# Hybrid mLSTM/HGRN2 decoder step on one core: Values' pieces placed by ScalarE, sample rows' output turned by VectorE, gates' sums in one product, margins for states, C batch split

## The chip, the cores and the metric

One core of a Trainium2 chip runs the whole layer as one program. The metric is the device time of one execution in microseconds (us). The engines are TensorE (PE; its weight loads are listed apart as PEld), VectorE (DVE), ScalarE (ACT), GpSimd (POOL) and SyncE (SP), whose queue issues nearly all transfers.

## The reference

One decoder layer is computed for 256 prompt tokens and for 8 samples of 8 tokens each, 320 tokens in all, with the same weights. Two mixers read one input projection; everything is in fp32.

```
proj = jnp.einsum('btd,de->bte', x, w_in)
(ml_q, ml_k, ml_v, ml_i, ml_f, ml_o, hg_q, hg_f, hg_i, hg_g, gate_a, gate_b) = jnp.split(proj, offs, axis=-1)
...
ig = (ml_i.astype(f32) + b_ig.astype(f32)).transpose(0, 2, 1)
lf = jax.nn.log_sigmoid(ml_f.astype(f32) + b_fg.astype(f32)).transpose(0, 2, 1)
h, C, n, m = _mlstm(q, k, v, ig, lf, C0, n0, m0)
h = _unheads((h - mu) * lax.rsqrt(var + LN_EPS)) * ml_norm_g
branch_a = h * jax.nn.sigmoid(ml_o)
...
o, S = _hgrn2(hq, jnp.log(f), 1.0 - f, _heads(hg_i, HG_HEADS), S0)
o = _unheads(o * lax.rsqrt(jnp.mean(jnp.square(o), axis=-1, keepdims=True) + LN_EPS)) * hg_norm_g
branch_b = o * jax.nn.silu(hg_g)
ya = jnp.einsum('btv,vd->btd', branch_a, w_branch_a)
yb = jnp.einsum('btv,vd->btd', branch_b, w_branch_b)
merged = jax.nn.sigmoid(gate_a) * ya + jax.nn.sigmoid(gate_b) * yb
x1 = _layernorm(DEEPNORM_ALPHA * x + jnp.einsum('btd,de->bte', merged, w_out), ln1_g, ln1_b)
hid = jnp.square(jax.nn.relu(jnp.einsum('btd,df->btf', x1, w_up)))
y = _layernorm(DEEPNORM_ALPHA * x1 + jnp.einsum('btf,fd->btd', hid, w_down), ln2_g, ln2_b)
```

The mLSTM has 4 heads (key width 256, value width 512), the HGRN2 mixer 8 heads (128 and 256). The final matrix states C and S are outputs as well, for the prompt (from zero) and for each sample (from a given state).

## The kernel before

All values are kept transposed, features on the 128 partitions and the 320 tokens along the row (256 prompt tokens, then 64 sample tokens). The dense projections are 304 tiles of 128 output features. A tile is 48 matmuls that add up in one PSUM bank: 16 slices of the contraction, three matmuls each, because weights and inputs are split into a high and a low part of type fp32r (high times high, high times low, low times high). Weights stream through three raw buffers `wr` of 512 KB, two units to a tile; ScalarE copies a unit to its high part `wh` and VectorE subtracts that to get `wl` (line 501), three prepared buffers in all. In the later stages tile `bb` gives five more pairs. TensorE runs these tiles one after the other (`run_main`).

Everything else is side work, written as generators (`m_...` for the mLSTM, `h_...` for HGRN2, `ev_...` for what is done with a finished tile). A planner (`Sched`) fixes each engine's order ahead of time, while the program is built: it keeps an estimated clock for each engine, and after every three matmuls of a tile it lets each generator put its next instruction into an engine's queue if its inputs should be there by then, up to 900 ns of side work on TensorE at a time. Estimated costs are written at the yields (`act(n)`, `dve(n)`, `pe_f(n)`); an event's `t` is the time at which something is thought to be there. On the chip each engine works its list in that order and waits on semaphores for inputs.

The pieces that the change touches:

- `rows` (line 782) makes the mLSTM's gates. Eight input and forget gates were summed in four partial rows by matmuls; two products with a 4-column selector (`sel`, lines 799 and 800) add these up, input gates in one bank, forget gates in another.
- `turn` (line 1152) turns a head's values (or HGRN2's inputs) from feature rows to token rows. It makes 24 VectorE transposes of 32x32 blocks a call, 16 for the prompt (line 1163) and 8 for the samples (line 1166), each reading 32 partitions and writing 32 others. It is called by `m_V` for 4 heads and by `h_i` for 8.
- `m_sample` and `h_out` end with a head's sample rows. The normalised output (`hb[:, 2, :]`, 128 by 512, or `on[:, 2, :]`, 128 by 256; only 64 of the 128 rows are real, 16 in every 32) is transposed on TensorE, four (line 1219) or two (line 1647) blocks of 128x128, copied from PSUM by ScalarE into token order and sent to a scratch tensor in DRAM (`hL`, `oL`) by one transfer. Prompt rows go another way already: a VectorE transpose in place and four transfers (`place`) that put 32x32 blocks where they belong.
- `ev_o` and `ev_hg` fetch these rows back (`fetch`) and multiply a gate by the norm's weight and by the row, one VectorE instruction each (lines 1704 and 1741).
- `m_states` and `h_load` load the samples' states, 256 and 512 KB a transfer; `m["parts"]` and `m["sat"]` are the times at which TensorE's batch that reads them (`PE_C`, `PE_H`) may be planned.
- `m_C` (line 1116) makes the prompt's final C after the last tile: for each head and half a batch of six matmuls of 512 columns, put into the queue as one piece. The first batch may go before the last norm's sums are done; the others wait for `ln[1]["fin"]`, which `ln_final` posts after its products for the sum and the sum of squares (lines 1842 and 1843). `ln_scale` and `y` then finish the output: 16 subtractions (line 1981) and 16 multiplications (line 1988) on VectorE, a ScalarE pass each, and transfers of `y`. `h_S` makes the final S, whose results are copied by ScalarE and VectorE (line 1616) and sent in four transfers.

Of the kernel before, what the change touches and what calls it, by code (L numbers as in the profile page):

```python
# [8 lines left out]
F32 = mybir.dt.float32  # L9
# [11 lines left out]
TOK = 320  # L21
# [56 lines left out]

C_ID, C_TRI, C_BM, C_SEL, C_SC, C_END = 0, 128, 256, 320, 328, 968


def constants():
# [8 lines left out]
    for r in range(4):  # L91
        c[r::32, C_SEL + r] = 1.0
        c[r + 4::32, C_SEL + 4 + r] = 1.0
    start = np.zeros(TOK, bool)
# [30 lines left out]
PE_OUT = 200.0  # L125
PART = 122.0
PE_LAT = 450.0

# [124 lines left out]
def acq(pool, n=1):  # L253
    return ("acq", pool, n)
# [63 lines left out]
class Program:  # L318
    def __init__(self, tc, nc, d, pools):
# [15 lines left out]
        self.f1 = p.tile([128, 10240], F32, name="f1", tag="f1")  # L335
        self.f2 = p.tile([128, 5232], F32, name="f2")
        self.f3 = p.tile([128, 5120], F32, name="f3", tag="f3")
# [29 lines left out]
    def carve(self):  # L367
# [58 lines left out]
        self.ats = Pool([self.ats0])  # L426
        self.sg = Pool([Part(self.f2, 4912)(320), self.tst2])
        B = Part(self.f2, 4176)
# [7 lines left out]
    def carve_h(self):  # L436
        C = self.Part(self.pool.tile([128, 5120], F32, name="f3h", tag="f3"))
        qz = C(256)
        self.hqz = Pool([qz])
        self.hyk = Pool([C(128)])  # L440
        for x in (qz, self.ats0, self.hkz0.bitcast(F32), *(y[0:64, 2, :] for y in self.it2)):
            self.nc.gpsimd.memset(x, 0.0)
        X, R = self.Part(self.pool.tile([128, 4096], F32R, name="rxb", tag="rx")), self.Part(self.ra)
        self.bah = Slices([(X if j < 12 else R)(TOK) for j in range(KT)])
        self.bal = Slices([R(TOK) for _ in range(KT)])
        now = self.s.t["pe"]
        self.hs.free += [(now, C(2048)), (now, self.hs3)]
        self.sb.free += [(now, C.three(4, 256)) for _ in range(2)]
        self.sg.free += [(now, self.f2[:, 4912:5232]), (now, self.late[0])]
        self.sr.free.append((now, self.late[1]))  # L450
        self.ld = Pool(self.late[2:])
# [330 lines left out]
    def rows(self, b):  # L782
# [10 lines left out]
        emg = row(128)  # L793
        sel = self.cst[:, C_SEL:C_SEL + 8]
# [9 lines left out]
        yield ("dve", dve(T, True), lambda: v.tensor_scalar(fx, p2[0:4, :T], bf, None, ALU.add))  # L804
        yield rel(self.sbank, p1)
        yield rel(self.sbank, p2)
        yield ("act", act(T), lambda: self.A(ax, fx, AF.Abs))
# [308 lines left out]
    def m_C(self, h):  # L1116
# [8 lines left out]
        for c in range(2):  # L1125
            if h or c:
                yield wait(self.ln[1]["fin"])
            b = yield acq(self.mbank)
            yield ("pe", 6 * pe_r(512), lambda: [self.mm(
                b, k.rearrange("p x s k -> p (x s k)")[:, 512 * x + 256 * c + 128 * s:512 * x + 256 * c + 128 * s + 128], w[:, y, s, :], start=n == 0, stop=n == 5)  # L1130
                for n, (s, x, y) in enumerate((s, x, y) for s in range(2) for x, y in ((0, 0), (0, 1), (1, 0)))])
            if c == 1:
# [19 lines left out]
    def turn(self, to, x):  # L1152

        v = self.nc.vector
        n = x.shape[1]
        for a in range(4):
            p = slice(32 * a, 32 * a + 32)
            col = lambda y: y.rearrange("p (c a k) -> p a c k", a=4, k=32)[:, a]
            for b in range(4):
                q = slice(32 * b, 32 * b + 32)  # L1160
                i = x[p, :, 0:NP_].rearrange("p c (i b k) -> p b i c k", b=4, k=32)[:, b]
                o = to[q, 0:2, :].rearrange("p i (c a k) -> p a i c k", a=4, k=32)[:, a]
                yield ("dve", dve_t(64 * n), lambda: v.transpose(o, i))  # L1163
            for b in range(2):
                o, i = col(to[64 + 32 * b:96 + 32 * b, 2, :]), x[p, :, NP_ + 32 * b:NP_ + 32 * b + 32]
                yield ("dve", dve_t(32 * n), lambda: v.transpose(o, i))

# [5 lines left out]
    def m_sample(self, h):  # L1173
# [42 lines left out]
        yield rel(self.sm, dn)  # L1216
        b = yield acq(self.sbank)
        for j in range(4):
            yield ("pe", PE_T, lambda: nc.tensor.transpose(b[:, 128 * j:128 * j + 128], hb[:, 2, 128 * j:128 * j + 128], self.ident))  # L1219
# [9 lines left out]
        yield rel(self.tst, o)  # L1229
        yield wait(m["hb_"])  # L1230
# [17 lines left out]
    def m_states(self, h):  # L1248
# [3 lines left out]
        for n in range(2 * NB):  # L1252
# [3 lines left out]
            m["cbs"].append(cb)  # L1256
            m["parts"][n].t = t
        yield post(m["ld"])
# [222 lines left out]
    def h_i(self, h):  # L1481
# [11 lines left out]
        hi, lo = vst[64:128, 0, :], vst[0:64, 0, :]  # L1493
        yield ("act", act(256), lambda: self.A(hi, it[64:128, 2, :]))
        yield ("dve", dve(256), lambda: v.tensor_tensor(lo, it[64:128, 2, :], hi.bitcast(F32), ALU.subtract))
        yield post(m["I"])
# [8 lines left out]
    def h_load(self, h):  # L1505
# [11 lines left out]
        m["sat"] = Ev()  # L1517
        m["sat"].t = t

# [102 lines left out]
    def h_out(self, h):  # L1622
# [21 lines left out]
        yield rel(self.at, at)  # L1644
        b = yield acq(self.sbank)
        for j in range(2):
            yield ("pe", PE_T, lambda: nc.tensor.transpose(b[:, 128 * j:128 * j + 128], on[:, 2, 128 * j:128 * j + 128], self.ident))  # L1647
        o = yield acq(self.ho)
        for j in range(2):
            yield ("act", act(64, True), lambda: self.A(by_row(o, 64 * j, False), by_row(b, 128 * j, True)))  # L1650
        yield rel(self.sbank, b)
        yield ("sp", 620, lambda: self.dma(
            self.oL[h].rearrange("(j p) t -> p j t", p=128), o[:, 0:128].rearrange("p (j t) -> p j t", t=64)))
        for j in range(2):
            yield post(self.oT_ev[2 * h + j])
        yield wait(self.later())
        yield rel(self.ho, o)
        yield wait(done)
# [34 lines left out]
    def fetched(self, kind, j):  # L1693
        yield wait(self.got[kind, j])
        return self.met[kind, j]

    def ev_o(self, j, c, b):
        v = self.nc.vector
# [4 lines left out]
        x = yield from self.fetched("o", j)  # L1703
        yield ("dve", dve(TOK, ptr=1), lambda: v.scalar_tensor_tensor(g, g, self.vec[:, V_MLG + j:V_MLG + j + 1], x, ALU.mult, ALU.mult))
        yield rel(self.ld, x)
# [26 lines left out]
    def ev_hg(self, j, c, b):  # L1732
# [7 lines left out]
        x = yield from self.fetched("hg", j)  # L1740
        yield ("dve", dve(TOK, ptr=1), lambda: v.scalar_tensor_tensor(g, g, self.vec[:, V_HGG + j:V_HGG + j + 1], x, ALU.mult, ALU.mult))
        yield rel(self.ld, x)
# [354 lines left out]
```

## Time and profile before

| | |
|---|---|
| median of 3 runs | 2295.86 us (2295.74 to 2296.64) |
| the profiled execution | 2296.11 us |
| its span | 2294.3 us |
| TensorE busy, instructions | 2285.9 us, 15592 |
| VectorE busy | 1458.0 us (64%) |
| ScalarE busy | 1036.4 us (45%) |
| transfers | 424.95 MB, mean 185 GB/s |

The span is the time that the profile covers; 1.8 us of the execution lie around it. A matmul of plain fp32 appears as two instructions (two passes), one of fp32r and a TensorE transpose as one. Matmuls overlap: the time that one takes from the stream is read from the distance between the starts of the weight loads (PEld) behind it, not from its own duration.

### The profile page before, as it was taken

Reading aid. Unit: us, or ns where it says so; the run is one execution under the profiler, and the core shown is the slowest. Engines: PE = TensorE matmul, PEld = TensorE weight load, DVE = VectorE, ACT = ScalarE, POOL = GpSimd, SP = SyncE. Lnnn points to the kernel's source line nnn. Section 1 sums busy time; section 2 is a strip of 40 time slices with the busy share of each in tenths; the row PEclk is TensorE's granted clock in tenths of the full one; section 3 lists DMA queues with packets and bytes.
Section 4 is the critical chain, followed back from the end, with each engine's and each line's share of the span. In section 5 each row is a group of like instructions: output and inputs, shape, how many; then the busy total and the mean of one; then the engine's idle time right before and its main releaser. Section 6 shows DMA issues by size and latency. Waiting matters only on the chain.

```text
span 2294.3 us, 38944 instructions
## 1 busy us (share of the span) xinstructions
PE 2285.9 (100%) x15592; PEld 2245.2 (98%) x15592; DVE 1458.0 (64%) x2626; ACT 1036.4 (45%) x1653; POOL 13.4 (1%) x37
## 2 busy tenths in 40 slices
PE   9999999999999999999999999999999999999998
PEld 9999998999999999999999999999999999999998
DVE  6786787788888886555555767544444444444455
ACT  5443444555555565444434446533442343234334
POOL 0000000000000000000000000000000000000000
PEclk9999999999999999999999999999999999999999
DMA  7578878665566655555555644444444444444476
GB/s 287 179 224 272 283 230 284 211 188 186 193 191 192 189 181 181 180 171 171 174 175 185 201 161 145 148 154 148 148 155 148 147 152 152 147 150 154 147 229 194
DMA packets 214575, 424.95 MB, mean 185 GB/s; under 512 B 83572, under 2 KB 110068, under 8 KB 213368
## 3 DMA queue, kind: packets, MB, share of 16 engines
q1 hardware_dynamic: 209512, 415.97, 55.4%
q0 software_dynamic: 4736, 6.29, 1.2%
q8 instruction: 122, 2.00, 0.3%
q14 instruction: 61, 0.50, 0.1%
q10 hardware_dynamic: 144, 0.20, 0.0%
HBM read 371.48 MB, written 50.90 MB: 184 GB/s over the span
## 4 chain that ended last, share of the span: by engine, by line
PE 98%; DVE 1%; ACT 1%; issue 0%; DMA 0%; ACTq 0%; DVEq 0%
PE bank L360 97%; DVE f3m L1981 0%; DVE f3m L1988 0%; ACT wh L354 0%; DVE wl L501 0%; DMA f<-first 0%; ACT f L354 0%; ACT f3m L354 0%; PE bank L1034 0%; DVE f L1163 0%; PE bank L1537 0%; PE bank L1219 0%; PE bank L1647 0%; ACT xh L354 0%; DVE ra L971 0%
## 5 line engine op out<-in xcount | busy, mean ns | idle before, releaser
L360 PE MATMUL bank<-xh,wh 128*128 128x320 f32 (+1 forms) x2504 | 796.1, 318 | 0.1
L360 PE MATMUL bank<-xh,wl 128*128 128x320 f32 (+1 forms) x2504 | 774.6, 310 | 0.0
L501 DVE TENSOR_TENSOR wl<-wr,wh 128x1024 fp32r<-128x1024 f32 x440 | 538.8, 1225 | 367.0 <-ACT wh L354 364.7
L360 PE MATMUL bank<-xl,wh 128*128 128x320 f32 (+1 forms) x2504 | 771.8, 309 | 0.0
L354 ACT ACTIVATE wh<-wr 128x1024 fp32r<-128x1024 f32 x440 | 465.6, 1058 | 533.3 <-PE bank L360 506.8
L360 PEld LDWEIGHTS bank<-xh,wh 128*128 128x128 f32 x2504 | 471.2, 188 | 17.6 <-issue 15.5
L360 PEld LDWEIGHTS bank<-xl,wh 128*128 128x128 f32 x2504 | 471.3, 188 | 3.4
L360 PEld LDWEIGHTS bank<-xh,wl 128*128 128x128 f32 x2504 | 471.5, 188 | 0.5 <-DVE wl L720 0.3
L501 DVE TENSOR_TENSOR bb<-wr,bb 128x1024 fp32r<-128x1024 f32 x162 | 198.5, 1225 | 194.2 <-ACT bb L354 193.9
L354 ACT ACTIVATE bb<-wr 128x1024 fp32r<-128x1024 f32 x162 | 171.6, 1059 | 294.8 <-PE bank L360 276.7
L360 PE MATMUL bank<-ra,wh 128*128 128x320 f32 x1008 | 275.9, 309 | 0.7 <-DVE ra L1678 0.7
L360 PE MATMUL bank<-ra,bb 128*128 128x320 f32 x1096 | 255.2, 309 | 0.0
L360 PE MATMUL bank<-xh,bb 128*128 128x320 f32 (+1 forms) x1136 | 253.8, 309 | 0.0
L360 PE MATMUL bank<-rxb,bb 128*128 128x320 f32 x1088 | 249.0, 308 | 0.0
L360 PEld LDWEIGHTS bank<-xh,bb 128*128 128x128 f32 x1136 | 191.0, 188 | 0.0
L360 PE MATMUL bank<-rxb,wl 128*128 128x320 f32 x608 | 187.6, 308 | 0.0
L360 PE MATMUL bank<-rxb,wh 128*128 128x320 f32 x608 | 187.5, 308 | 0.0
L360 PEld LDWEIGHTS bank<-ra,bb 128*128 128x128 f32 x1096 | 184.9, 187 | 0.0
L360 PEld LDWEIGHTS bank<-rxb,bb 128*128 128x128 f32 x1088 | 184.2, 187 | 0.0
L360 PEld LDWEIGHTS bank<-ra,wh 128*128 128x128 f32 x1008 | 180.9, 187 | 0.9 <-DVE ra L1678 0.9
L360 PE MATMUL bank<-xl,bb 128*128 128x320 f32 (+1 forms) x568 | 175.5, 309 | 0.0
L360 PE MATMUL bank<-bb,wh 128*128 128x320 f32 (+1 forms) x536 | 119.0, 313 | 0.0
(259 smaller groups left out, 2239.7 us busy)
## 6 DMA issues: line engine op xcount, KB each, us to landing
wr<-wt SPq DMA_DIRECT2D x602, 512.0 KB, 3.3
rx<-C SPq DMA_DIRECT2D x34, 256.0 KB, 4.6
Cs<-rx SPq DMA_DIRECT2D x34, 256.0 KB, 4.9
f<-C SPq DMA_DIRECT2D x30, 256.0 KB, 5.4
Cs<-f SPq DMA_DIRECT2D x30, 256.0 KB, 4.8
f<-first SPq DMA_DIRECT2D x6, 704.0 KB, 9.4
vD<-ra SPq DMA_DIRECT2D x4, 1024.0 KB, 6.4
f<-S SPq DMA_DIRECT2D x8, 512.0 KB, 5.6
```

The source lines that it names most:

```text
L354: return self.nc.scalar.activation(out, in_, func, **kw)
L360: self.nc.tensor.matmul(*a, **kw)
L501: self.V().tensor_tensor(lo, raw, hi.bitcast(F32), ALU.subtract)
```

## The change

- `rows`: the selector becomes 128 columns wide, input gates in columns 0 to 3, forget gates in 32 to 35, so that one product gives both sums in one bank.
- `turn`: one VectorE transpose of the whole tile in place, 128 partitions wide, then 24 ScalarE copies that put the 32x32 blocks into place.
- Sample rows: one VectorE transpose in place of 128x512 or 128x256, and four transfers (`place`) in pieces of 16 values straight from there. The TensorE transposes, ScalarE's copies and the single transfer go. The scratch rows now stand in another token order, which the new `join` undoes while it multiplies: one instruction for the prompt and two of 32 columns for the samples in place of one.
- `STATE`: 1200 ns more until a state is taken as there, in the plan only.
- `m_C`: a batch of six is put into the queue as two of three, and of the first batch only the first three go before `fin`.
- `h_i`: two planned costs rise by 122 ns (`PART`).
- `f2` shrinks by 28 columns, by which the constants grow.

```diff
-C_ID, C_TRI, C_BM, C_SEL, C_SC, C_END = 0, 128, 256, 320, 328, 968
+C_ID, C_TRI, C_BM, C_SEL, C_SC, C_END = 0, 128, 256, 320, 356, 996
...
+STATE = 1200.0
...
-        p1, p2 = yield acq(self.sbank, 2)
-        yield ("pe", pe_f(T), lambda: self.mm(p1[0:4, :T], sel[:, 0:4], gs, start=True, stop=True))
-        yield ("pe", pe_f(T), lambda: self.mm(p2[0:4, :T], sel[:, 4:8], gs, start=True, stop=True))
+        p1 = yield acq(self.sbank)
+        yield ("pe", pe_f(T), lambda: self.mm(p1[:, :T], sel, gs, start=True, stop=True))
...
+            for s in range(2):
+                if s and not h and not c:
+                    yield wait(self.ln[1]["fin"])
+                yield ("pe", 3 * pe_r(512), lambda: [self.mm(
+                    b, k.rearrange("p x s k -> p (x s k)")[:, 512 * x + 256 * c + 128 * s:512 * x + 256 * c + 128 * s + 128], w[:, y, s, :],
+                    start=s == 0 and n == 0, stop=s == 1 and n == 2) for n, (x, y) in enumerate(((0, 0), (0, 1), (1, 0)))])
...
+        t = yield ("dve", dve_t(TOK * n), lambda: v.transpose(x, x))
...
-                yield ("dve", dve_t(64 * n), lambda: v.transpose(o, i))
+                yield ("act", act(64 * n) + PART, lambda: self.A(o, i), (t,))
...
-                yield ("dve", dve_t(32 * n), lambda: v.transpose(o, i))
+                yield ("act", act(32 * n) + PART, lambda: self.A(o, i), (t,))
+
+    def sample_to(self, home):
+
+        return lambda a: cap2(home, 16 * a, [[64, 32], [32 * 64, home.shape[0] // 32], [1, 16]])
...
-        b = yield acq(self.sbank)
-        for j in range(4):
-            yield ("pe", PE_T, lambda: nc.tensor.transpose(b[:, 128 * j:128 * j + 128], hb[:, 2, 128 * j:128 * j + 128], self.ident))
-        o = yield acq(self.tst)
-        for j in range(4):
-            yield ("act", act(64, True), lambda: self.A(by_row(o, 64 * j, False), by_row(b, 128 * j, True)))
-        yield rel(self.sbank, b)
-        yield ("sp", 620, lambda: self.dma(
-            self.hL[h].rearrange("(j p) t -> p j t", p=128), o[:, 0:256].rearrange("p (j t) -> p j t", t=64)))
+        yield ("dve", dve_t(512), lambda: v.transpose(hb[:, 2, :], hb[:, 2, :]))
+        yield from self.place(self.sample_to(self.hL[h]), hb[:, 2, :].rearrange("p (c j) -> p c j", j=32)[:, :, 0:16])
...
-            m["parts"][n].t = t
+            m["parts"][n].t = t + STATE
...
-        m["sat"].t = t
+        m["sat"].t = t + STATE
...
+    def join(self, g, w, x):
+
+        v = self.nc.vector
+        yield ("dve", dve(NP_, ptr=1), lambda: v.scalar_tensor_tensor(g[:, 0:NP_], g[:, 0:NP_], w, x[:, 0:NP_], ALU.mult, ALU.mult))
+        z = x[:, NP_:TOK].rearrange("p (x y t) -> p y x t", x=4, y=2)
+        for y in range(2):
+            s = g[:, NP_ + 32 * y:NP_ + 32 * y + 32].rearrange("p (x t) -> p x t", x=4)
+            yield ("dve", dve(32, ptr=1), lambda: v.scalar_tensor_tensor(s, s, w, z[:, y], ALU.mult, ALU.mult))
```

`h_out` changes for `oL` as `m_sample` does for `hL`. What follows are places in the engines' lists, in the order that the planner now gives them; a row names the line, the operation, what it writes and reads, and the shape.

TensorE before, where the first mLSTM head's sample rows are turned (`cst` is the identity, `f_77` the output rows, `bank_83` a tile's bank):

```order
L360 MATMUL bank_83<-xh,wl 128x320
L1219 MATMUL bank_86<-cst,f_77 128x128
L360 MATMUL bank_83<-xh,wh 128x320
L360 MATMUL bank_83<-xl,wh 128x320
L360 MATMUL bank_83<-xh,wl 128x320
L360 MATMUL bank_83<-xh,wh 128x320
L360 MATMUL bank_83<-xl,wh 128x320
L360 MATMUL bank_83<-xh,wl 128x320
L1219 MATMUL bank_86<-cst,f_77 128x128
```

SyncE's list after, where the same rows leave (`Cs`, `C` and `rx` belong to the states, `wr` is the next unit of weights):

```order
L364 DMA hL_199<-f_77 32x16x16 x2
L364 DMA wr<-wt 128x1024
L364 DMA hL_199<-f_77 32x16x16
L364 DMA Cs<-rx 128x512
L364 DMA hL_199<-f_77 32x16x16
L364 DMA rx<-C 128x512
```

The four transposes stand between a tile's matmuls, one each after six; in the new list TensorE has none of them, and the rows leave by four transfers among which loads of weights and states stand.

ScalarE's list after, where the first head's values are turned (`f_75` the values, `wh` the weights' high part, `bank_83` a finished tile):

```order
L355 ACTIVATE wh<-wr 128x1024
L355 ACTIVATE f_75<-f_75 32x8x32 x4
L355 ACTIVATE f_75<-f_75 32x4x32 x2
L355 ACTIVATE f_75<-f_75 32x8x32
L355 ACTIVATE wh<-wr 128x1024
L355 ACTIVATE f_75<-f_75 32x8x32 x3
L355 ACTIVATE f_75<-f_75 32x4x32 x2
L355 ACTIVATE f_75<-bank_83 128x320
L355 ACTIVATE f_75<-f_75 32x8x32
L355 ACTIVATE wh<-wr 128x1024
```

Up to seven pieces stand between two copies of weights; before, these pieces were transposes in VectorE's list.

TensorE at the end, before (`bb,ones` sums for the last norm, `bb,wh` the first batch for C, `f3m,ones` and `f_76,ones` the norm's last two products):

```order
L360 MATMUL bank_84<-bb,ones 128x320
L360 MATMUL bank_88<-bb,wh 128x512 x6
L360 MATMUL bank_86<-f3m,ones 128x320
L360 MATMUL bank_84<-f_76,ones 128x320
L360 MATMUL bank_85<-bb,wh 128x512 x6
```

and after:

```order
L361 MATMUL bank_88<-bb,ones 128x320
L361 MATMUL bank_86<-bb,wh 128x512 x3
L361 MATMUL bank_87<-f3m,ones 128x320
L361 MATMUL bank_88<-f_76,ones 128x320
L361 MATMUL bank_86<-bb,wh 128x512 x3
L361 MATMUL bank_81<-bb,wl 128x512 x3
```

Three of the six matmuls have moved behind the norm's two products.

More of the change, by code (lines that the diff above doesn't have):

```diff
@@ L92, in constants @@
         c[r::32, C_SEL + r] = 1.0
-        c[r + 4::32, C_SEL + 4 + r] = 1.0
+        c[r + 4::32, C_SEL + 32 + r] = 1.0
     start = np.zeros(TOK, bool)
@@ L335, in __init__ @@
         self.f1 = p.tile([128, 10240], F32, name="f1", tag="f1")
-        self.f2 = p.tile([128, 5232], F32, name="f2")
+        self.f2 = p.tile([128, 5204], F32, name="f2")
         self.f3 = p.tile([128, 5120], F32, name="f3", tag="f3")
@@ L448, in carve_h @@
         self.sb.free += [(now, C.three(4, 256)) for _ in range(2)]
-        self.sg.free += [(now, self.f2[:, 4912:5232]), (now, self.late[0])]
+        self.sg.free += [(now, self.f2[:, 4884:5204]), (now, self.late[0])]
         self.sr.free.append((now, self.late[1]))
@@ L793, in rows @@
         emg = row(128)
-        sel = self.cst[:, C_SEL:C_SEL + 8]
+        sel = self.cst[:, C_SEL:C_SEL + 128]
         yield ("sp", 620, lambda: self.dma(m0, self.d["m0"]))
@@ L1644, in h_out @@
         yield rel(self.at, at)
[L1645 to L1653, printed above, removed]
+        yield ("dve", dve_t(256), lambda: v.transpose(on[:, 2, :], on[:, 2, :]))
+        yield from self.place(self.sample_to(self.oL[h]), on[:, 2, :].rearrange("p (c j) -> p c j", j=32)[:, :, 0:16])
         for j in range(2):
@@ L1703, in ev_o @@
         x = yield from self.fetched("o", j)
-        yield ("dve", dve(TOK, ptr=1), lambda: v.scalar_tensor_tensor(g, g, self.vec[:, V_MLG + j:V_MLG + j + 1], x, ALU.mult, ALU.mult))
+        yield from self.join(g, self.vec[:, V_MLG + j:V_MLG + j + 1], x)
         yield rel(self.ld, x)
@@ L1740, in ev_hg @@
         x = yield from self.fetched("hg", j)
-        yield ("dve", dve(TOK, ptr=1), lambda: v.scalar_tensor_tensor(g, g, self.vec[:, V_HGG + j:V_HGG + j + 1], x, ALU.mult, ALU.mult))
+        yield from self.join(g, self.vec[:, V_HGG + j:V_HGG + j + 1], x)
         yield rel(self.ld, x)
```

14 lines of the change are left out of this document (4 added, 10 removed).

## The prediction

> **What bounds the kernel now.** First the page's busy times, the chain that ended last, and, from the table by stage, one long stretch without side work (busy time and count of PE, PEld, DVE, ACT and POOL, then granted clock, share of the transfer engines and GB/s).
>
> ```profile
> PE 2285.9 (100%) x15592; PEld 2245.2 (98%) x15592; DVE 1458.0 (64%) x2626; ACT 1036.4 (45%) x1653; POOL 13.4 (1%) x37
> PE 98%; DVE 1%; ACT 1%; issue 0%; DMA 0%; ACTq 0%; DVEq 0%
> 1500.00:2000.00 500.00, 500.00 (x3414) 500.00 (x3413) 224.83 (x253) 178.99 (x211) 0.00 (x0) 1.00 0.45 150
> ```
>
> TensorE is busy all the time and is 98% of the chain. A tile's matmul takes 500/3414 = 0.146 us of its stream, and the granted clock is 1.00, so nothing is to be had from the clock. What the chain can lose is (a) side work in TensorE's list, (b) waits in that list, (c) the end, after the last tile. For (b) the waits of the weight loads:
>
> ```profile
> PEld bank L360 <- issue: 25.9, 82, 0.8
> PEld bank L360 <- DMA rx<-C: 1.2, 3, 0.6
> PEld bank L360 <- DVE ra L1678: 0.9, 1, 0.9
> PEld bank L360 <- DVE ra L971: 0.8, 1, 0.8
> PEld bank L360 <- ACT wh L354: 0.6, 2, 0.3
> ```
>
> Real waits, without the first row (it waits for nothing shown), are some 4 us in all: relieving VectorE or ScalarE can give only a few tenths here and there. So each edit is priced by what it takes from TensorE's list, and every other cost counts only if TensorE comes to wait for it.
>
> **Sample rows without TensorE.** 4 heads by 4 and 8 heads by 2 transposes go.
>
> ```profile
> L1219 PE MATMUL bank<-cst,f 128*128 128x128 f32 x16 | 4.3, 272 | 0.0
> ...
> 173.10 0.14 PEld L1219 LDWEIGHTS bank<-cst,f 128*128 128x128 f32 x1
> 173.25 0.19 PEld L360 LDWEIGHTS bank<-xh,wh 128*128 128x128 f32 x1
> 173.36 0.19 PEld L360 LDWEIGHTS bank<-xl,wh 128*128 128x128 f32 x1
> ```
>
> The 272 ns is a duration with overlap, not the price. A load starts when the load before it has been taken into use, that is when the matmul ahead has streamed; so the transpose's own share is the distance of the two loads behind it: 173.36 - 173.25 = 0.11 us. 32 times 0.11 = **3.5 us**, all on the chain; if each cost its whole spacing of a tile's matmul (0.146) it would be 4.7. I take 3.5. The new VectorE transposes, 4 of 128x512 and 8 of 128x256, and `join`'s 64 more instructions lie beside TensorE (VectorE is at 64%). That the rows now take another way to DRAM costs nothing, because they lie there long before they are fetched:
>
> ```profile
> L363 SPq DMA_DIRECT2D f<-hL x16: 457/464/1204, 760.3 to 878.4; - x16
> L363 SPq DMA_DIRECT2D hL<-f x4: 378/980/1162, 179.9 to 413.1; - x4
> ```
>
> The last of the mLSTM's is issued at 413.1 and the first fetched at 760.3. Without that cover `ev_o` would wait for the landing, some us, with its gate in hand.
>
> **Gates' sums.** Two products become one.
>
> ```profile
> 30.95 0.19 PEld L360 LDWEIGHTS bank<-xh,wl 128*128 128x128 f32 x1
> 31.33 0.09 PEld L360 LDWEIGHTS bank<-f,cst 128*4 128x4 f32 x2 [0.19 <-issue]
> 31.96 0.19 PEld L360 LDWEIGHTS bank<-xh,wh 128*128 128x128 f32 x1 [0.54 <-issue]
> 32.07 0.19 PEld L360 LDWEIGHTS bank<-xl,wh 128*128 128x128 f32 x1
> ...
> 2270.33 0.42 PEld L360 LDWEIGHTS bank<-f3m,ones 128*128 128x128 f32 x2
> 2270.83 0.46 PEld L360 LDWEIGHTS bank<-f,ones 128*128 128x128 f32 x2
> 2271.36 1.39 PEld L360 LDWEIGHTS bank<-bb,wh 128*128 128x128 f32 x6
> ```
>
> From 30.95 to 32.07 are 1.12 us, in which two tile matmuls (0.29) and one product run: the narrow product costs 0.83, and 0.73 of idle loads stands before and behind it. The last norm's products have the new form (plain fp32, 128 columns, 320 wide): 2271.36 - 2270.83 = 0.53, with no such idle. So 2 x 0.83 - 0.53 = **1.1 us**. If the new product kept the idle time it would be 0.8, which is the lower bound; that the idle is a cost of narrowness is inferred from these two forms. `ig` and `fx` then read one bank, which hides beside the tiles.
>
> **Margins for states.**
>
> ```profile
> 381.72 0.12 PEld L360 LDWEIGHTS bank<-f 128*32 128x32 f32 x2 [0.31 <-issue]
> 382.63 0.14 PEld L360 LDWEIGHTS bank<-rx,f 128*32 128x32 f32 x2 [0.55 <-DMA rx<-C]
> ```
>
> Between passes of such a batch 0.31 us of idle is normal; at 382.63 a state came late by 0.24. The margin puts the batch 1.2 us later in the plan and removes this: **0.2 us**, bounds 0 and 1.2 (the whole row above).
>
> **Values' pieces.** VectorE loses 24 short transposes a call and gets one; ScalarE gets 24 pieces.
>
> ```profile
> L1163 DVE STREAM_TRANSPOSE f<-f 32x256 f32<-32x256 f32 x64 | 27.9, 436 | 1.5
> L1097 DVE STREAM_TRANSPOSE f<-f 128x512 f32<-128x512 f32 x8 | 5.7, 708 | 0.2
> L354 ACT ACTIVATE rh<-f 64x256 fp32r<-64x256 f32 x8 | 3.3, 415 | 1.6 <-DVE f L1166 1.5
> L354 ACT ACTIVATE ra<-f 64x128 fp32r<-64x128 f32 x4 | 1.2, 307 | 0.1
> L501 DVE TENSOR_TENSOR wl<-wr,wh 128x1024 fp32r<-128x1024 f32 x440 | 538.8, 1225 | 367.0 <-ACT wh L354 364.7
> L354 ACT ACTIVATE wh<-wr 128x1024 fp32r<-128x1024 f32 x440 | 465.6, 1058 | 533.3 <-PE bank L360 506.8 <-issue 16.6 <-DMA wr<-wt 6.7
> ```
>
> A whole-tile transpose isn't in the trace; by 708 ns for 512 columns and about 1 ns a column more, 1280 columns are some 1.5 us, against 16 x 0.436 and 8 of about 0.3 = 9 us. The pieces' nearest rows are 0.415 and 0.307: 16 x 0.415 + 8 x 0.307 = 9.1 us of ScalarE a head of values. On the chain this is nothing, as long as weights come in time: ScalarE's copies of weights waited 506.8 us for TensorE to free a prepared buffer, so they run ahead as far as buffers allow. A unit lasts TensorE 24 x 0.146 = 3.5 us; in it ScalarE has one copy (1.06) and up to seven pieces (2.8) and a tile's evacuation now and then (0.44), so 3.9 to 4.3, for about four units. It falls behind by some 2 us and has a lead of two units less 2.4 us of preparation (1.06 and 1.23, with the hand-over), 4.6 us. In the 8 HGRN2 heads the pieces are half as wide. What does change is the one wait for `ra L971`: there TensorE waited 0.8 us for VectorE, which was behind with the first head's transposes. With these gone VectorE is early; I take half, **0.4 us**, bounds 0 (the wait moves to ScalarE) and 0.8.
>
> **C batch split.** The end, in order of time:
>
> ```profile
> 2269.03 1.25 PEld L360 LDWEIGHTS bank<-bb,wh 128*128 128x128 f32 x6
> 2269.22 0.49 DVE L1961 TENSOR_TENSOR f3m<-f3m,bank 128x320 f32<-128x320 f32 x1 [4.52 <-PE bank L360]
> 2269.81 0.47 ACT L354 ACTIVATE f<-f3m 128x320 f32<-128x320 f32 x1 [6.03 <-DVE f3m L1961]
> ...
> 2272.17 0.48 DVE L1857 SCALAR_TENSOR_TENSOR f<-bank,f 128x320 f32<-128x320 f32 x1
> ...
> 2286.17 1.70 PEld L360 LDWEIGHTS bank<-xls 128*128 128x128 f32 x8
> 2288.19 0.74 DVE L1616 COPY oS<-bank 128x256 f32<-128x256 f32 x2
> 2289.39 0.45 SPq L363 DMA_DIRECT2D y<-f3m  x1
> 2289.93 0.41 SPq L363 DMA_DIRECT2D Sp<-oS  x1
> ```
>
> The last tile's row is ready at 2269.71, its square at 2270.28, but the products start at 2270.33 and 2270.83, behind six matmuls. With three (0.7 us) they can start at about 2269.8 and 2270.35: the norm's chain, L1857 and the VectorE run behind it come 0.5 to 0.7 us earlier. What ends last is then TensorE's last products for S: their copies cannot start before 2288.2 whatever the norm does, since the list holds the same work. They need some 0.4 more for the last pair's second half, so the copies end 0.3 us earlier than 2288.93. The last transfer, at 2289.93, stood behind two copies and the `y` before it, which now leaves earlier; it can gain up to 1.1. I take **0.8 us**, bounds 0.3 and 1.1.
>
> **The sum.** 3.5 + 1.1 + 0.2 + 0.4 + 0.8 = 6.0 us. The profiled execution took 2296.11 us (span 2294.3 and 1.8 around it), so 2290.1; the median of the runs stands 0.25 lower, at 2295.86, so **2289.9 us**. Other waits are taken to stay.
>
> **Rivals.** *New waits take it back.* The planner gives TensorE's list anew, and a side product put 0.5 us too early stops the tiles, as the 0.8 us at `ra L971` does. For it: sixteen updates, eight batches and all `spread` products move. Against it: only two single waits of that size stand in the list above, with 1000 side instructions on TensorE (15592 less 304 x 48). Three new ones of 0.8, and the old one kept: 2289.9 + 2.4 + 0.4 = 2292.7, within 0.2%.
>
> *Pieces hold up the weights, and it is slower.* ScalarE works in order, so a weight copy stands behind seven pieces. With a piece at p us a turn costs 24 p + 5 x 1.06, against 5 x 3.5 + 4.6 that TensorE allows: it decides from p = 0.70, and the kernel is slower than before by over 0.2% from p = 0.81, where 4 heads lose 10.6 us. At p = 0.9 TensorE waits 4.8 us in each of 4 heads, 19 us: 2309. Against it: 0.415 for twice the partitions with the same columns.
>
> *Small pieces in DRAM.* These transfers write 64-byte pieces; the prompt's rows (`hH`) go in 128-byte ones.
>
> ```profile
> wr<-wt SPq DMA_DIRECT2D x602, 512.0 KB, 3.3
> hH<-f SPq DMA_DIRECT2D x16, 128.0 KB, 3.8
> hL<-f SPq DMA_DIRECT2D x4, 128.0 KB, 4.6
> ```
>
> They share the queue with the weights, whose lead is about 12 us (five units of 3.5 in buffers, less 3.3 to land and 2.4 of preparation). If a transfer of 32 KB in 64-byte pieces took four times the 3.8 us that 128 KB take here, 15 us, weights would come 3 us late in 12 heads: 36 us, 2326. The rows speak against: pieces half as long, but a quarter of the bytes, half as many pieces. The Trainium skill (DMA: Bandwidth & Descriptors, Specifications) says that transfers below 512 bytes lose line rate because the engine then reads, modifies and writes; by that rule this edit, from 256-byte pieces to 64-byte ones, is the wrong way round. The trace does not bear it out: `hL` in 256-byte pieces lands in 4.6 us, `hH` in 128-byte ones with as many bytes in 3.8; no run yet shows 64 bytes.
>
> *Nothing but the end's bound.* If the end gives 0.3 and the waits nothing, the gain is 4.9: 2291.0, still inside the forecast's own range, 2288.4 to 2291.3.
>
> **How the numbers follow.** About 0.2% (4.6 us) is what a measurement of this kernel can tell from no change. TensorE's own savings, 3.5 + 1.1, alone make that, and hang on no wait. Forecast 78%; new waits 14%; pieces 5%; small transfers 3%. The range for 8 in 10: below, all upper bounds, 3.5 + 1.1 + 1.2 + 0.8 + 1.1 = 7.7, so 2288.2, taken to 2288.0; above, into the new waits, 2293.0. Faster by over 0.2%: 0.78; within: 0.14; slower: 0.08.
>
> **What would show it.** No L1219 and L1647, and one `f,cst` of 128 columns without idle loads around it. `DMA rx<-C` and `DVE ra L971` gone from the waits. The pieces at 0.41 and 0.31 us, and TensorE's waits for `ACT wh` no longer than 0.6 us in all. `hL` landing in under 5 us. L1857 0.5 to 0.7 us nearer to the last tile and the last transfer 0.3 to 1.1 nearer. The forecast is wrong if TensorE's busy time falls by less than 4 us, or if new rows in its waits add up to over 1.5 us.

## The result and the profile after

| | before | after |
|---|---|---|
| median of 12 runs each | 2296.35 us (2295.58 to 2297.69) | 2302.18 us (2296.82 to 2308.67) |
| ratio after / before | | 1.0024, 95% interval 1.0016 to 1.0032 |
| the profiled execution (span) | 2296.11 us (2294.3) | 2300.11 us (2298.3) |

The kernel became slower, by 0.24%, where 6 us less were forecast. The profiled execution is faster than the changed kernel's median; what its slower ones, up to 2308.67 us, lost more is not on record. The page of the changed kernel, busy time and count of each engine, and the chain that ended last:

```profile
PE 2284.0 (99%) x15558; PEld 2241.8 (98%) x15558; DVE 1377.9 (60%) x2426; ACT 1121.8 (49%) x1909; POOL 13.5 (1%) x37
PE 97%; DMA 1%; DVE 1%; ACT 1%; SPq 0%; issue 0%; ACTq 0%; DVEq 0%
```

TensorE has 34 instructions fewer, but its busy time falls by only 1.9 us, and transfers, 0% of the chain before, are now 1%. The waits of its weight loads (us in total, times, longest) name the transfer:

```profile
PEld bank L361 <- DMA rx<-C: 8.0, 4, 3.5
PEld bank L361 <- DVE rx L1277: 1.2, 1, 1.2
...
PEld bank L361 <- DVE ra L1669: 0.9, 1, 0.9
PEld bank L361 <- ACT wh L355: 0.6, 2, 0.3
```

`DVE ra L971` is gone as forecast, and `ACT wh` has not grown. `DMA rx<-C`, three waits of 1.2 us in all before, is 8.0: TensorE has come in its list to a product on one of the samples' mLSTM states, and the state is not there. The three long ones lie at 182, 259 and 341 us, in the first state batches of the second, third and fourth head. The chain of waits through the first of them (start, us, what), and the weight load behind it in the timeline:

```profile
172.68 1.03 SPq L364
...
175.12 0.45 SPq L364
...
175.61 4.96 DMA Cs<-rx
...
180.59 5.54 DMA rx<-C
...
186.18 3.91 PE bank L361 x19
```

```profile
186.18 0.14 PEld L361 LDWEIGHTS bank<-rx,f 128*32 128x32 f32 x2 [3.52 <-DMA rx<-C]
```

An updated state is stored (`Cs<-rx`), only then is its buffer free, and the next head's state is loaded into it (`rx<-C`): 4.96 + 5.54, with the hand-over 10.57 us from the store's issue to the product. The planner counts on 1500 ns + bytes/380 + 600 ns for a transfer (`transfer`, in the code of `Sched`), 2.79 us for 256 KB. Twice that and the new margin of 1.2 are 6.8 us. The difference, 3.8, is about the wait of 3.52. In the other two long waits no store ends the chain, but one load alone, issued behind other transfers in SyncE's list; TensorE was ready for the state 2.9 and 3.4 us after its issue:

```profile
256.21 4.76 DMA rx<-C
...
261.02 2.02 PE bank L361 x8
...
337.89 5.24 DMA rx<-C
...
343.17 1.79 PE bank L361 x7
```

What the transfers take on the chip stands on the page (count, KB each, median us from issue to landing), first before, then after:

```profile
rx<-C SPq DMA_DIRECT2D x34, 256.0 KB, 4.6
Cs<-rx SPq DMA_DIRECT2D x34, 256.0 KB, 4.9
```

```profile
rx<-C SPq DMA_DIRECT2D x34, 256.0 KB, 5.1
Cs<-rx SPq DMA_DIRECT2D x34, 256.0 KB, 4.6
f<-C SPq DMA_DIRECT2D x30, 256.0 KB, 5.4
hL<-f SPq DMA_DIRECT2D x16, 32.0 KB, 4.5
oL<-f SPq DMA_DIRECT2D x32, 16.0 KB, 2.5
```

The medians are 1.8 to 2.6 us above the planner's 2.79 for 256 KB, in both kernels. From 200 to 400 us the transfer engines are 0.80 and 0.85 busy (the column before the last; the last is GB/s):

```profile
200.00:300.00 100.00, 90.08 (x664) 1.00 0.80 256
300.00:400.00 100.00, 91.21 (x667) 1.00 0.85 262
```

The Trainium skill (DMA: Bandwidth & Descriptors, Anatomy of one DMA) fits one transfer, on GpSimd's path, as about 2.0 us and its bytes at 436 GB/s; by that 256 KB are 2.6 us, near the planner's figure and half of what these rows show. The Trainium skill (DMA: Bandwidth & Descriptors, Latency and other measured facts) has access to memory slower under high load; how much of the 5.1 us is load, no run here separates.

Where the other differences lie is read from the start of the same weight load of the tiles in both traces, first load of the tile that the column names, counted from 0 (the kernel of the row minus the kernel before, us):

| kernel | tile 1 | tile 4 | tile 118 | last tile | whole span |
|---|---|---|---|---|---|
| after | +0.32 | -0.77 | +3.12 | +3.17 | +4.0 |
| gates' sums and C batch alone | +0.43 | -0.68 | +0.43 | +0.49 | +0.8 |
| after, with the landing time corrected in the plan | +0.50 | -0.59 | -6.45 | -6.38 | -6.6 |
| the same, sample rows as before | +0.49 | -0.59 | -3.11 | -3.05 | -3.2 |
| before, with the landing time corrected | +0.30 | +0.32 | -0.87 | -0.86 | -0.8 |

The gates' product lies before tile 4, the last side work of the mixers before tile 118; from there to the last tile nothing moves by more than 0.08 us. The differences come to rest by 870 us, so all else that was won and lost lies before that, and in the changed kernel 0.8 us more were lost after the last tile.

### The profile page after: what moved, and what is told of

The parts are those of the page before. It is cut to its first block, busy times and chain, and to the rows that moved or that the text cites. A ratio compares the mean times of both kernels' runs of the same rounds, so it can differ in the third digit from the quotient of the medians.

```text
span 2298.3 us, 38972 instructions
## 1 busy us (share of the span) xinstructions
PE 2284.0 (99%) x15558; PEld 2241.8 (98%) x15558; DVE 1377.9 (60%) x2426; ACT 1121.8 (49%) x1909; POOL 13.5 (1%) x37
## 4 chain that ended last, share of the span: by engine, by line
PE 97%; DMA 1%; DVE 1%; ACT 1%; SPq 0%; issue 0%; ACTq 0%; DVEq 0%
PE bank L361 96%; DMA rx<-C 1%; DMA f<-first 0%; SPq L364 0%; ACT f3m L355 0%; DMA Cs<-rx 0%; DVE wl L502 0%; ACT wh L355 0%; ACT oC L355 0%; DVE f3m L1981 0%; DVE rx L1277 0%; PE bank L1536 0%; DVE f3m L1988 0%; PE bank L1033 0%; ACT f L355 0%
## 5 line engine op out<-in xcount | busy, mean ns | idle before, releaser
L355 ACT ACTIVATE f<-f 128x320 f32<-128x320 f32 (+6 forms) x413 | 152.7, 370 | 33.6 <-DVE f L1315 17.1
```

What stands on the lines that cost most here:

```text
L355: return self.nc.scalar.activation(out, in_, func, **kw)
```

## The experiments

Theories: **P**, with values' pieces off VectorE the plan calls for states earlier than store, buffer and load can follow. **Q**, the four transfers of sample rows crowd SyncE's queue. **R**, any new plan loses some us by chance. All kernels were compared with runs of the kernel before on the same chip.

**The rows back on TensorE** (`e1`), **the pieces back on VectorE** (`e2`), **margins of 6000 and 0 ns** (`e3`, `e4`), each in the changed kernel:

```diff
 e1: m_sample, h_out, ev_o, ev_hg as before
 e2 (turn):
-        t = yield ("dve", dve_t(TOK * n), lambda: v.transpose(x, x))
...
-                yield ("act", act(64 * n) + PART, lambda: self.A(o, i), (t,))
+                yield ("dve", dve_t(64 * n), lambda: v.transpose(o, i))
...
 e3 / e4:
-STATE = 1200.0
+STATE = 6000.0   /   STATE = 0.0
```

> All of the change but the sample rows, which go as before (TensorE transposes, one transfer a head, one multiplication on fetching). TensorE's list has the state batches at the same tiles as in the changed kernel. Theory Q (the four transfers a head stand in SyncE's list ahead of the last state loads and make them late): TensorE's wait for DMA rx<-C falls from 8 us to under 1.5, and the kernel is faster than before by the gates, the end and the states, some 2 us: 2294. Theory P (the values' pieces on ScalarE let the plan call for states sooner than stores and loads can turn round): the wait stays at 5 to 8 us and the time goes up by the transposes, 3.5 us, to 2303 to 2306.

> All of the change but the values' pieces, which VectorE transposes as before. Q: the wait for DMA rx<-C stays at 4 us or more, time 2298 to 2303. P: the wait falls under 1.5 us and the savings on TensorE show, 2290 to 2292.

> The changed kernel with a margin of 6000 ns for states in place of 1200. Q and P alike say that the batches come too early in the list by up to 4 us; with 6 us they find their states: wait for DMA rx<-C under 1 us, 2290 to 2292. If the loop of store and load as such is too slow for TensorE, the wait moves to the next batch and the time stays above 2296.

> The changed kernel without any margin for states. Batches come 1.2 us earlier in the list than in the changed kernel, so each late state costs about 1.2 us more: Q and P, wait for DMA rx<-C 10 to 14 us and 2303 to 2308. If the margin itself moved the batches to a worse place, the wait falls.

Measured: `e1` 2298.48 us, 1.0011 (1.0001 to 1.0020); `e2` 2296.47, 1.0001 (0.9991 to 1.0011; one execution of its ten, of 3728.7 us, is left out of the ratio); `e3` 2294.49, 0.9994 (0.9984 to 1.0003); `e4` 2302.17, 1.0031 (1.0020 to 1.0041). The waits of `e1`, `e2`, `e3` and `e4`, in this order:

```profile
PEld bank L361 <- DMA rx<-C: 5.1, 5, 1.9
```

```profile
PEld bank L361 <- DVE f L1276: 4.5, 2, 2.7
...
PEld bank L361 <- DVE ra L970: 0.8, 1, 0.8
```

```profile
PEld bank L361 <- DVE f L1315: 2.2, 1, 2.2
...
PEld bank L361 <- DVE f L1424: 1.0, 1, 1.0
```

```profile
PEld bank L361 <- DMA rx<-C: 10.4, 6, 3.2
```

With the rows back the states still come late, by less; the waits are in the range that P gave, but the time lies between the two that P and Q gave. With the pieces back the states are not late, but then TensorE waits for VectorE, 4.5 us at the state updates (line 1276), and the wait for `ra` is there again, so the savings don't show. A margin of 6000 ns removes the waits for states whole; without any margin they are 10.4 us. The gain that 6000 ns left, 1.4 us against the runs before on that chip, is not told from none by its interval and less than the 4 to 6 expected; 3.2 us of waits for VectorE had turned up at 842 us, among HGRN2's products.

**One part at a time on the kernel before** (`f1` the pieces, `f2` the rows, `f3` the gates' sums and the C batch), and **6000 ns for the mLSTM's states alone** (`f4`):

```diff
 f1: turn as in the change, nothing else
 f2: m_sample, h_out, join as in the change, nothing else
 f3: rows, m_C as in the change, nothing else
 f4 (after; m_states with 6000 ns):
-        m["sat"].t = t + STATE
+        m["sat"].t = t + 1200.0
```

> The kernel before with one part of the change: values' pieces on ScalarE (one VectorE transpose of the whole tile, 24 copies a call), nothing else. Theory P (with the pieces off VectorE the plan calls for the states earlier than store, buffer and load can follow): TensorE waits for `DMA rx<-C`, as in the changed kernel without margins (10.4 us there), here 4 to 10 us; the wait for `ra L971` goes; time 3 to 9 us above the kernel before. Theory Q (four sample-row transfers a head crowd SyncE's queue): no such wait, time within 1 us of before. Theory R (any new plan loses some us by chance): a loss too, but in other rows of the waits than `rx<-C`.

> The kernel before with one part of the change: sample rows turned by VectorE and placed by four transfers, with the join, nothing else. Theory P: states come as before (1.2 us of `rx<-C` waits), 32 transposes of 0.11 us are off TensorE, so 3.5 us below the kernel before, less what VectorE, still with the values' pieces, is late for (4.5 us of `f L1276` waits in the kernel with the turn as before): 0 to 3.5 us below. Theory Q: `rx<-C` waits of 3 us or more, time equal to before or above. Theory R: some us of waits in any row.

> The kernel before with two small parts of the change: the gates' sums in one product and the C batch in two halves. By the prediction's terms 1.1 us at the sums and 0.3 to 1.1 at the end, 1.4 to 2.2 below the kernel before; if the end gives nothing, 1.1 (in the changed kernel the copies of S ended 0.2 us earlier after the last tile, but the last transfer did not). Theories P and Q: the waits stay as before. Theory R: some us lost in new waits, since the plan is a new one from the first tile on.

> The changed kernel with a margin of 6000 ns for the mLSTM's states alone; HGRN2's keep 1200. Theory P: no wait for `rx<-C`, as with 6000 for both; if the 3.2 us of waits for `f L1315` and `f L1424` at 842 us there came from HGRN2's margin, they are gone and the time is 2289 to 2290, else 2292 to 2293. Theory Q: as with 6000 for both, since the transfers are the same.

Measured: `f1` 2300.02, 1.0017 (1.0008 to 1.0027), waits for `rx<-C` 5.6 us; `f2` 2295.81, 0.9997 (0.9988 to 1.0006), waits 3.8 us; `f3` 2296.34, 1.0000 (0.9991 to 1.0009), waits 2.1 us; `f4` 2294.30, 0.9993 (0.9983 to 1.0003).

```profile
PEld bank L361 <- DMA rx<-C: 5.6, 2, 3.1
```

`f1` is as P has it: the pieces alone, with no extra transfer, make the states late and the kernel slower. `f2` speaks against P as the whole cause: with the pieces still on VectorE, its new plan has states late too. Its profile is of its slowest execution (2298.10 us), so 3.8 is probably more than an execution at its median waits. `f3` points to the reason: it leaves all eight state batches at the tiles where they were, and its waits still are 2.1 us against 1.2; it is 1.1 us ahead from the gates on and loses 1.3 between tiles 40 and 43, where its longest wait (1.6) lies. So the list of before had no slack there, as far as one trace of each can show. `f4` was a miss: the waits at 842 us stayed (2.2 and 1.0 us). In the traces every engine's list in `f4` is that of `e3`, row by row, so HGRN2's margin moved nothing and `f4` is `e3` measured again, on another chip (2294.30 and 2294.49 us).

**The plan put right in two ways** (`g1` the landing time, `g6` a margin of 9000 ns), and **the rows on GpSimd's queue** (`g2`; `g9` with 9000 ns too):

```diff
 g1 (after; STATE = 0):
-        self.lands.append(self.wire + 600.0)
+        self.lands.append(self.wire + 2900.0)
 g6 (after): m_states with 9000 ns, HGRN2's 1200
 g2 (after; sample rows only), g9 with the margins of g6 as well:
-            yield ("sp", 620, lambda: self.dma(to(a), x[32 * a:32 * a + 32]))
+            self.nc.gpsimd.dma_start(to(a), x[32 * a:32 * a + 32])
...
+            yield ("pool", 620, lambda: go(a))
```

> The changed kernel with no margin for states; in its place the planner's landing time of every transfer is 2.3 us later (600 ns become 2900 after the bytes), so that a state of 256 KB is planned to land 5.1 us after its issue, as the profile of the changed kernel shows, and not 2.8. Theory P: the margin was a stand-in for half of this error, and the buffers' release after a store has the same error, so the waits for `rx<-C` go: 0 to 1.5 us, time 2289 to 2293. Theory Q: the four transfers of sample rows still stand among the loads and stores on SyncE's queue, 3 us of `rx<-C` waits and 2295 or more. Theory R (any new plan loses by chance): waits of some us in other rows.

> The changed kernel, but the four transfers of sample rows a head are issued by GpSimd, which is idle, instead of SyncE; TensorE's list has the state batches at the same tiles to within 0.2 (11.9, 14.4, 21.9, 25.2, 30.8, 34.4, 40.2, 43.9). Theory Q: SyncE's queue is free of them, the waits for `rx<-C` fall from 8.0 to 4 us or less, time 2297 to 2299. Theory P: the batches are called as early as before, so the waits stay at 6 to 10 us, time 2300 to 2303. If both hold, about 5 us as with the rows back on TensorE (5.1).

> The changed kernel with a margin of 9000 ns for the mLSTM's states alone. HGRN2's batches then stand in TensorE's list at the same tiles as in the changed kernel (53.2 to 96.7), not as with 6000 ns (53.8 to 102.6), where TensorE waited 3.2 us for VectorE at 842 us. Theory P: no wait for `rx<-C`, none at 842 us, and the gain of the parts that take work from TensorE comes out: 2290 to 2292. Theory Q: `rx<-C` waits of 1 to 3 us remain, 2292 to 2295. Theory R: waits of 3 us or more in another row.

> Sample rows' transfers on GpSimd's queue and a margin of 9000 ns for the mLSTM's states. Theory P: the queue matters little once the margin covers the landing, so the time is within 1 us of the same margin with the rows on SyncE's queue. Theory Q: 1 to 3 us below it, since weights and states no longer stand behind sample rows.

Measured: `g1` 2290.23, 0.9973 (0.9962 to 0.9984); `g2` 2300.11, 1.0015 (1.0005 to 1.0025); `g6` **2289.53**, 0.9970 (0.9958 to 0.9982); `g9` 2290.29, 0.9973 (0.9963 to 0.9983). The waits of `g1`, of `g6` and of `g2`:

```profile
PEld bank L361 <- DVE ra L1669: 0.9, 1, 0.9
...
PEld bank L361 <- DMA rx<-C: 0.5, 2, 0.3
```

```profile
PEld bank L361 <- ACT wh L355: 1.5, 3, 0.8
...
PEld bank L361 <- DVE ra L1669: 0.9, 1, 0.9
```

```profile
PEld bank L361 <- DMA rx<-C: 7.8, 4, 4.3
```

With a landing time as measured, or with a margin that covers it, the waits for states are gone but for 0.5 us and a gain of the forecast's size is there. `g2` speaks against Q: with the batches at the same tiles to 0.2 and SyncE free of the small transfers the waits are 7.8 against 8.0, and with the longer margin the queue makes 0.8 us between the medians, the other way. A share of 2 us is not excluded, since the intervals of `g2` and of the changed kernel overlap. No wait of 1 us or more came in place of the old ones (the longest for `ACT wh` in `g6` is 0.8), against R.

**Whose gain it is**: the landing time of `g1` in the kernel before (`h1`), in the changed kernel with the rows as before (`h2`) and with the pieces as before (`h3`).

```diff
 h1 (before), h2 (e1, STATE = 0), h3 (e2, STATE = 0):
-        self.lands.append(self.wire + 600.0)
+        self.lands.append(self.wire + 2900.0)
```

> The kernel before with nothing but the planner's landing time of a transfer put 2.3 us later (600 ns become 2900). Theory P (the changed kernel lost its gain only to states that came late in a plan that believed them early): the waits of 1.2 us for `rx<-C` go and nothing else is gained, 2295 to 2297. Rival: the better plan by itself brings most of the 6 us that the changed kernel shows with the same landing time, and the change's parts little: 2290 to 2292.

> The changed kernel with the later landing time in the plan (2290.2), but sample rows and the join as before. Theory P: 32 transposes come back on TensorE at 0.11 us each and no wait for states, so 3.5 us above, 2293.7. Rival (the better plan does it): 2290 to 2291.

> The changed kernel with the later landing time in the plan (2290.2), but values' turn as before, on VectorE. Theory P: no wait for states; VectorE has the pieces again, so it is late as in the kernel before (`ra L970`, 0.8 us) or as with the turn as before and the old landing time (5.3 us): 2291 to 2295. Rival (the better plan does it): 2290 to 2291.

Measured: `h1` 2295.08, 0.9994 (0.9984 to 1.0004); `h2` 2292.67, 0.9983 (0.9973 to 0.9992); `h3` 2295.65, 0.9998 (0.9988 to 1.0007). The corrected plan alone takes 0.9 of the 1.2 us of waits from the kernel before and gains 1.2 between the medians, not told from no change by its interval. The rows are worth 2.4 us between the medians of `h2` and `g1`, 3.3 at the last tile. Without the pieces' move little of the gain is left, since VectorE, which has the pieces and the rows' transposes and joins, is late again. In the profiled execution of `h3`, its slowest, TensorE also pauses once for 2.3 us after the last tile, for which the profile names no releaser. The waits for VectorE in `h3`:

```profile
PEld bank L361 <- DVE f L1314: 1.8, 1, 1.8
...
PEld bank L1535 <- DVE f L993: 0.9, 1, 0.9
...
PEld bank L361 <- DVE f L1423: 0.6, 1, 0.6
```

All kernels in one table; "planned" is the time from a C state's issue to its use in the plan (2.8 us, or 5.1 with the corrected landing, and the margin), "shortest" the shortest time in the trace from the issue of such a load (`rx<-C`, 34 of them) to TensorE being ready for the state (loads and products taken in their order), "waits" TensorE's for `rx<-C` in the same execution, whose time stands under "profiled". The kernel before, run beside each group, had medians of 2295.88 to 2296.42.

| kernel | pieces on | planned | shortest, us | waits, us | profiled, us | median, us |
|---|---|---|---|---|---|---|
| before | VectorE | 2.8 | 3.9 | 1.2 | 2296.11 | 2296.35 |
| f3 | VectorE | 2.8 | 3.9 | 2.1 | 2296.92 | 2296.34 |
| f2 | VectorE | 2.8 | 3.3 | 3.8 | 2298.10 | 2295.81 |
| e2 | VectorE | 4.0 | 6.8 | none | 2296.33 | 2296.47 |
| e1 | ScalarE | 4.0 | 3.9 | 5.1 | 2298.51 | 2298.48 |
| f1 | ScalarE | 2.8 | 2.9 | 5.6 | 2299.28 | 2300.02 |
| g2 | ScalarE | 4.0 | 2.2 | 7.8 | 2302.21 | 2300.11 |
| after | ScalarE | 4.0 | 2.1 | 8.0 | 2300.11 | 2302.18 |
| e4 | ScalarE | 2.8 | 2.3 | 10.4 | 2301.20 | 2302.17 |
| h1 | VectorE | 5.1 | 7.6 | 0.3 | 2295.24 | 2295.08 |
| h3 | VectorE | 5.1 | 7.3 | none | 2297.26 | 2295.65 |
| h2 | ScalarE | 5.1 | 7.8 | 0.2 | 2292.95 | 2292.67 |
| g1 | ScalarE | 5.1 | 7.6 | 0.5 | 2289.67 | 2290.23 |
| f4 | ScalarE | 8.8 | 7.6 | none | 2296.24 | 2294.30 |
| e3 | ScalarE | 8.8 | 8.8 | none | 2294.05 | 2294.49 |
| g6 | ScalarE | 11.8 | 12.6 | none | 2290.23 | 2289.53 |
| g9 | ScalarE | 11.8 | 11.8 | none | 2289.93 | 2290.29 |

P holds in a wider form: the plan puts the load of a state too near to its use. Every kernel that waits over 1 us has loads that TensorE needs 2.1 to 3.9 us after their issue, while such loads take 4.5 to 6.0 us to land in the median of their traces; where the shortest time is 6.8 us or more, 0.5 us of waits are left at most. Moving the pieces is what shortens it: between `e2` and the changed kernel, which differ in the pieces alone, it falls from 6.8 to 2.1, between the kernel before and `f1` from 3.9 to 2.9. It is not the tile at which a batch stands: with the pieces on ScalarE the last batch moves from tile 45.8 to 43.9, but in `g6` it stands at 42.5 and its states are in time, and in `f2`, where no batch stands earlier than before, two states are late.

Two things stay open. Rows back on TensorE (`e1`) had 2.9 us less of these waits than the changed kernel with the batches at the same tiles; `g2` speaks against the queue as the reason, and one trace of each cannot tell whether it is more than the transfers' spread. And what makes VectorE late at 842 us with 6000 ns but not with 9000 was not tried; the two plans place HGRN2's batches at other tiles.

## Why the prediction was wrong

The step that failed is **"Other waits are taken to stay."**, together with the term for the margins. The waits for `rx<-C` were priced as a remainder of 1.2 us that a margin could only shorten (0.2 us); in the changed kernel they are 8.0. They were the visible end of loads without slack. The rows that showed it stood on the page of before, in its table of transfers (4.6 us for `rx<-C`, 4.9 for `Cs<-rx`), beside a planner that believed 2.8; the prediction set neither against the other. It had the mechanism as its first rival, "a side product put 0.5 us too early stops the tiles", but sized it by the waits of before, three of 0.8 us, at 14%; the waits were up to 3.5 us, in the largest of them a store and a load late one behind the other, in two more a load alone (1.9 each). Both of its own signs of being wrong came out: new waits above 1.5 us, and a fall of TensorE's busy time below 4.

Term by term:

- **Transposes, 3.5 us**: right, as far as measured. The difference of the two corrected kernels with and without them (`h2`, `g1`) is 3.3 us at the last tile in their traces and 2.4 between their medians.
- **Gates' sums, 1.1 us**: right, also in its size. `f3` is 1.11 us earlier at tile 4 than at tile 1, and the new product shows no idle load around it:

```profile
31.27 0.19 PEld L361 LDWEIGHTS bank<-xh,wl 128*128 128x128 f32 x1
31.42 0.34 PEld L361 LDWEIGHTS bank<-f,cst 128*128 128x128 f32 x2
31.84 0.19 PEld L361 LDWEIGHTS bank<-xh,wh 128*128 128x128 f32 x1
32.10 0.19 PEld L361 LDWEIGHTS bank<-xl,wh 128*128 128x128 f32 x1
```

  From 31.27 to 32.10 are 0.83 us with two tile matmuls (0.29) in it: 0.54 for the product, 0.53 in the sum.
- **Margins, 0.2 us**: wrong in kind. 1.2 us did not cover the 2.3 by which one landing was believed too early (5.1 against 2.8), let alone two.
- **`ra L971`, 0.4 us**: the wait is gone whole, 0.8, and stays gone in all kernels with the pieces on ScalarE. The pieces' move is worth more than that, as cover: without it (`h3`) VectorE holds TensorE up by more than the wait of before.
- **The end, 0.8 us**: wrong. The norm's chain and the copies moved nearly as forecast, the last transfer did not (the first row is from before, the others from after):

```profile
2268.88 0.19 PEld L360 LDWEIGHTS bank<-bb,ones 128*128 128x128 f32 x1
```

```profile
2272.06 0.19 PEld L361 LDWEIGHTS bank<-bb,ones 128*128 128x128 f32 x1
...
2274.67 0.48 DVE L1857 SCALAR_TENSOR_TENSOR f<-bank,f 128x320 f32<-128x320 f32 x1
...
2290.37 1.76 ACT L355 ACTIVATE f3m<-f3m,vec 128x320 f32<-128x320 f32 x3
2291.07 1.87 SPq L364 DMA_DIRECT2D y<-f3m  x3
2291.49 0.42 DVE L1615 COPY oS<-bank 128x256 f32<-128x256 f32 x1 [0.40 <-PE bank L361]
2293.03 0.96 SPq L364 DMA_DIRECT2D Sp<-oS  x2
```

  From the last `bb,ones` load to L1857 are 2.61 us, before 3.29 (2272.17 - 2268.88): 0.68 earlier, as forecast. The last copy ends at 2291.91, 19.85 us after that load, before 20.05: 0.2 earlier, 0.3 forecast. But the last `Sp` is issued at 21.48, and at 21.07 to 21.16 in ten of the twelve other kernels with the split batch (later in `e4` and `h3`), against 21.04 to 21.05 in the four with the whole one. ScalarE, which makes a pass over each piece of `y`, works without a gap from 2283.05 on and ends its last pass 20.07 us after that load, before 20.12. The last `y` is issued 0.4 us earlier, but two `Sp` follow it on SyncE's queue where one did. The term is 0 in the kernels with the split batch; the 0.8 us that the profiled execution lost there is the issue of the last `Sp` (0.4) and the time from there to the end.
- **Pieces hold up the weights**: refuted as forecast. They take 0.415 and 0.307 us, the transpose of the whole tile 1.49 (1.5 estimated), and TensorE's waits for `ACT wh` are 0.6 us in all, as before:

```profile
L355 ACT ACTIVATE f<-f 32x128 f32<-32x128 f32 x128 | 39.4, 307 | 6.1 <-DVE f L1158 2.3 <-DVE misc L1066 2.0
L355 ACT ACTIVATE f<-f 32x256 f32<-32x256 f32 x64 | 26.5, 415 | 3.6 <-DVE f L1158 2.8
L1158 DVE STREAM_TRANSPOSE f<-f 128x1280 f32<-128x1280 f32 x4 | 6.0, 1488 | 0.0
```

- **Small pieces in DRAM**: refuted too. `hL` in 64-byte pieces lands in 4.5 us, under the 5 named.

With the states in time, 3.5 + 1.1 + 0.8 + 1.2 (the old waits) = 6.6 us, which is what the span of `g1` shows against before; 0.5 us of waits are left in it, so the match to a tenth is partly luck. The forecast of 2289.9 us is met by the kernels with the corrected plan, 2289.53 to 2290.29, not by the one that was forecast, and that too is partly luck: the end gave nothing of its 0.8, the waits gave more than the 0.2 and 0.4 taken. A slip in the working changes nothing: the forecast's own range runs to 2288.2 by its upper bounds, not to 2288.4.

## What to carry to other kernels

Where a list is planned ahead, set each time that the plan believes beside the same time on the page, transfers first: an error there can stay hidden as long as some other engine is late enough, and come out when that engine is relieved, as it did here. Small waits for a transfer, in several places alike, can mean that there is no slack and not that there is little to win. When work is taken from the busiest engine, ask which of its inputs arrived just in time before.

## What the runs showed that was not expected

- The kernels with the most waits for states also spread most: the changed kernel's 12 runs lie within 11.9 us, those of `e4` and `g2` within 5.7 and 6.8, those of the kernel before within 2.1, and of `g1` (7 runs) and `g6` (6 runs) within 1.4. These waits are not the only reason: `e3` and `h3`, which have none, spread by 3.7 and 3.3.
- A transfer of sample rows, 32 KB in 512 pieces of 64 bytes, takes as long (4.5 us) as the one of 128 KB in 512 pieces of 256 bytes took (4.6), and there are now four a head on the queue in place of one. The Trainium skill (DMA: Bandwidth & Descriptors, Specifications) says that below 512 bytes line rate is lost; a quarter of the bytes in the same time agrees with that, though both are below the bound and a fixed part of the time would show the same.
- GpSimd issued the same small transfers nearly as well as SyncE: in `g2`, `hL` landed in 5.1 us from its queue (4.5 from SyncE's), `oL` in 2.3 (2.5).
